# A hybrid transformer step on one core: load queues of the down phase, and the order of the first gate and up products

## The chip, the core and the metric

One core of a Trainium2 chip runs the whole kernel. The metric is the device time of one execution in microseconds (us). Its engines are TensorE (PE, with the weight loads PEld), VectorE (DVE), ScalarE (ACT), GpSimd (POOL) and SyncE (SP), each with its own instruction queue, worked off in order; they wait for one another by semaphores. DMA transfers are issued from an engine's queue (here SP, POOL and ACT) and carried by 16 DMA engines.

## The reference, cut to what matters

One layer for 512 prompt frames and 64 sample frames, 576 rows in all, D = 2048, FF = 5632, all in float32:

```
hn  = rmsnorm(x, g_norm1);  proj = hn @ w_in
mix = concat(stick-breaking attention (8 heads), gated short convolution), each normed
x   = x + mix @ w_out
h2  = rmsnorm(x, g_norm2)
y   = x + (silu(h2 @ w_gate) * (h2 @ w_up)) @ w_down
```

Outputs are y, the new keys and values and the new convolution state. The change lies in the last two lines, the feed-forward part (from about 930 us to the end).

## The kernel before

**Numbers in two parts.** Every float32 operand is held as a high part (cast to the matmul's fp32r form by ACT) and a low part (the difference, by DVE); `split` (L217, L218) makes both. A product of two operands takes three matmuls: high by high, low by high, high by low (`multiply`).

**Units.** The gate and up products are made of 42 units (numbers 0 to 41; a gate unit and an up unit for each pair of 128-wide frames of the hidden layer but the first, which the `wide` section does in the plain way). The down product has 36 units (42 to 77), listed in `DOWN`: unit (d, a, b) adds the hidden pairs a to b-1 to output column block d (256 wide), so a block is done in several units, and its running sum ("residual", x2) goes to DRAM after each unit and comes back for the next of that block. A unit is a 2 x 2 block product by Winograd's form of Strassen's method: seven products, called (n, p) for unit n and product p, of m pairs of 128 rows each, 3 m matmuls in each. A gate or up unit has m = 8, 24 matmuls in a product; a down unit m = 3 to 7.

**Order.** The matmuls run in a list written out by hand, `order`. Within a unit the products go 1, 2, 6, 7, 5, 3, 4, and product 1 of the next unit is put ahead of products 3 and 4 of this one. The operand of a product (weight columns or sums of them, L1050 to L1054, then `split` into `whl`) is prepared two products ahead (`AHEAD = 2`); DVE and ACT work in the order that the scheduler gave. Product 6 needs three sums of 128 x 1024 on DVE first. Results: products 1, 6, 5 and 3 of a unit pile up in the PSUM tile `psy`, whose states are copied out by ACT (`part`, L1074); product 2 is `psx`, 7 and 4 are `psw`. In a down unit DVE adds them to the residual tile (`add`, L1133).

**Loads.** Weights come from DRAM by SP (`load_weight`, L179) into two buffers each of `raw` and `raw2`; one unit ahead. A load waits until DVE and ACT have read the buffer. The three tiles of frames `h2a` (high, low) and `b22`, used by gate and up units, are reused in the down phase as three of seven slots; the other four slots are made when the down phase begins.

**Frames.** The frame sums (`frame_sums`, `tsum`) are made for the gate and up units while the wide section runs. Each hidden pair's seven forms are split by `put_form` (tile `form`, two buffers) and stored to `hid_dram` by POOL (L921, 288 KB each). The down phase loads a whole pair (seven forms, 2016 KB) back into a slot by SP (`load_pair`, L1139). Before, slots 0 to 3 are asked for at the start of unit 42, one more at the start of each of the next three units, and the others where `calls` says, after product 4 of a unit whose end frees slots: sometimes several at once.

**Residuals and outputs.** `load_x2` (L1124, 576 KB, SP) brings a unit's residual into one of two buffers at the start of the unit; `store_x2` (L1128, 576 KB, POOL) writes it after product 4. A load therefore waits for the store of two units before to land. The last unit of a block transposes its residual on PE and writes `ob` to the output by SP (L1155) and `obs` by ACT (L1162).

So in the down phase SP's queue holds weights, slots, residual loads and outputs, in program order; POOL's holds the form stores that are left from unit 41 and the residual stores.

Of the kernel before, what the change touches and what calls it, by code (L numbers as in the profile page):

```python
# [10 lines left out]
F32 = mybir.dt.float32  # L11
# [5 lines left out]
P = 128  # L17
# [3 lines left out]
HALF = T // 2  # L21
# [72 lines left out]
def tile_hybrid_stream_step(  # L94
# [6 lines left out]
    nc = tc.nc  # L101
# [5 lines left out]
    yp, ys = y_prompt[0], y_sample[0]  # L107
# [16 lines left out]
    specs = []  # L124
# [20 lines left out]
    NGU = len(UNITS)  # L145
# [26 lines left out]
        nc.scalar.copy(out=hi[:, a:b], in_=raw[:, a:b])  # L172
        lo_eng.tensor_tensor(out=lo[:, a:b], in0=raw[:, a:b], in1=hi[:, a:b].bitcast(F32), op=ALU.subtract)  # L173

    raws = []

    def load_weight():
        raw, raw3, src = weight_raw(len(raws))
        nc.sync.dma_start(out=raw3, in_=src)  # L179
        raws.append(raw)  # L180

    def split_weight(lo_eng):
        raw = raws[len(ready)]
# [175 lines left out]
    stores = []  # L359
    with tc.manual_schedule(engines={mybir.EngineType.Activation, mybir.EngineType.DVE, mybir.EngineType.SP}):  # L360
        raw, raw3, src = weight_raw(0)
        raws.append(raw)
        hi, lo = weight_split(0)
        w0h, w0l = ready[0]

        def load_w0(q):
            nc.sync.dma_start(out=raw3[:, 4 * q : 4 * q + 4, :], in_=src[:, 4 * q : 4 * q + 4, :])

        load_x(0)
        load_s(0)  # L370
        nc.sync.dma_start(out=g1raw, in_=g_norm1[0].rearrange("(r c) -> r c", c=P))
        load_x(1)
        load_x(2)
        load_w0(0)
        load_x(3)
        load_s(1)
        load_w0(1)
        load_x(4)
        load_s(2)
        load_x(5)  # L380
        load_w0(2)
        load_x(6)
        load_w0(3)
        load_weight()
        hi1, lo1 = weight_split(1)
        q0ps = [ps_pj.tile([P, HALF], F32, tag="pj", name="pj") for _ in HALVES]
        for kt in range(KD + LAG):
            if kt == 14:
                load_vectors()
            if kt == KD - 1:  # L390
                load_weight()
                for kt_, st in stores:
                    nc.sync.dma_start(out=xt_dram[kt_], in_=st)
                stores.clear()
            for sc, (k0, k1) in enumerate(SCH):
                if kt == k0:
                    pss, psc = turn_samples(sc), sc
            if kt == 0:
                psg = misc("ps_g1")
                nc.tensor.transpose(psg[:, :KD], g1raw, ident[:KD, :KD])  # L400
                nc.vector.tensor_copy(out=g1c, in_=psg[:, :KD])
            for c, (k0, k1) in enumerate(XCH):
                if k0 <= kt < k1:
                    turn_x(kt, c, kt - k0, psc, pss)
            if kt in (0, 4, 8, 12):
                weight_parts(raw, hi, lo, kt * P, (kt + 4) * P, nc.gpsimd if kt else nc.vector)
            if kt in (14, 16):
                a = (kt - 14) * 512
                weight_parts(raws[1], hi1, lo1, a, a + 1024, nc.gpsimd if kt == 14 else nc.vector)
            if kt >= 4 and not (kt >= 9 and kt % 2) and kt != 14 and squares and XCH[squares[0][0]][1] <= kt:  # L410
                square(*squares.pop(0))
            if kt >= LAG:
                for ps, (a, b) in zip(q0ps, HALVES):
                    step(ps, w0h, w0l, slice(0, P), xhi, xlo, kt - LAG, KD, a, b)
        pos[0] = 1
        while squares:
            square(*squares.pop(0))
        nc.sync.dma_start(out=xt_dram[KD - 1], in_=stores[0][1])
        turn_vectors()

        ssr = rpool.tile([P, 5], F32, name="ssr")
        nc.vector.reduce_sum(out=ssr, in_=ssx, axis=mybir.AxisListType.X)
        nc.vector.tensor_scalar(out=ssr, in0=ssr, scalar1=1.0 / D, scalar2=EPS, op0=ALU.mult, op1=ALU.add)
        rst = rpool.tile([P, 5], F32, name="rst")
        nc.gpsimd.tensor_tensor(out=rst, in0=ssr, in1=nhalf, op=ALU.pow)
# [467 lines left out]
    def frame_sums():  # L893

        for j in range(NP):
            ev, od = x2(2 * j), x2(2 * j + 1)
            ge, go = col("g2", 2 * j), col("g2", 2 * j + 1)
            pool, tag = (tpool, f"t{j}") if j < 4 else (ypool, f"y{j - 4}")
            b11 = tmp.tile([P, HALF], F32, tag="ms", name="b11", bufs=1)
            b22 = tmp.tile([P, HALF], F32, tag="t", name="b22", bufs=1)  # L900
            nc.scalar.activation(out=b11, in_=ev[:, :HALF], func=AF.Copy, scale=ge)
            nc.scalar.activation(out=b22, in_=od[:, HALF:], func=AF.Copy, scale=go)
            t = b12pool.tile([P, 4, HALF], F32, tag="ht", name="t")
            t1, t2, t3, t4 = (t[:, n] for n in range(4))
            nc.vector.scalar_tensor_tensor(out=t1, in0=ev[:, HALF:], scalar=ge, in1=b11, op0=ALU.mult, op1=ALU.subtract)
            nc.vector.tensor_tensor(out=t2, in0=b22, in1=t1, op=ALU.subtract)
            nc.vector.scalar_tensor_tensor(out=t3, in0=ev[:, HALF:], scalar=ge, in1=b22, op0=ALU.mult, op1=ALU.subtract)
            nc.vector.scalar_tensor_tensor(out=t4, in0=od[:, :HALF], scalar=go, in1=t2, op0=ALU.mult, op1=ALU.subtract)
            tt = pool.tile([P, 2, 4, HALF], F32R, tag=tag, name=f"tsum{j}")
            split(tt[:, 0], tt[:, 1], t)  # L910
            tsum.append(tt)
            yield 9

# [72 lines left out]

    pipe.spawn(frame_sums(), 20)
    wide("gate", row_scale2)
    load_weight()
    wide("up")  # L990
    pipe.flush()
    b12pool.release()
    blocks["pool"] = w2pool = tc.alloc_tile_pool(name="w2pool", bufs=1, reuse_waits="tile", side="left")
# [6 lines left out]
    slots = {}  # L1000
# [11 lines left out]
        return [(tsum[j][:, 0, q, :], tsum[j][:, 1, q, :]) for j in range(m)]  # L1012

    NU = len(UNITS)
    order = [(0, 1), (0, 2), (1, 1), (0, 6), (0, 7), (0, 5), (1, 2), (0, 3), (0, 4), (1, 6), (1, 7), (1, 5)]
    for n in range(1, NU):
        if n == NGU - 1:

# [13 lines left out]
    slot_turn = [0]  # L1032

    def column(i, m):
        while len(raws) <= i:
            load_weight()
        v = raws[i].rearrange("p (j s c) -> p j s c", s=2, c=P)
        return v[:, :, 0, :], v[:, :, 1, :]

# [81 lines left out]
    def load_x2(n):  # L1121
        d = UNITS[n][1]
        xt2[n] = down["pool"].tile([P, 2, T], F32, tag="x2", name=f"x2_{n}", bufs=2)
        nc.sync.dma_start(out=xt2[n], in_=x2_dram[2 * d : 2 * d + 2].rearrange("k p t -> p k t"))  # L1124

    def store_x2(n):
        d = UNITS[n][1]
# [7 lines left out]
    def load_pair(p):  # L1135
        tag = ("h2ah", "h2al", "b22", "s3", "s4", "s5", "s6")[p % SLOTS]
        pool = h2pool if p % SLOTS < 3 else down["pool"]
        slots[p] = pool.tile([P, FORMS, 2, HALF], F32R, tag=tag, name=f"slot{p}")
        nc.sync.dma_start(out=slots[p].bitcast(F32), in_=hid_dram[p])  # L1139

    def store_y(n, c, i):

        x2t, cs = xt2[n][:, c, :], slice((2 * UNITS[n][1] + c) * P, (2 * UNITS[n][1] + c + 1) * P)
        whole = (c, 1 - i) in unit[n].setdefault("done", set())
        unit[n]["done"].add((c, i))
        b0, b1 = ((0, 2), (3, 4), (0, 3), (2, 4))[2 * whole + i]

        def work():
            yield 3
            ob = down["pool"].tile([P, 3, P], F32, tag="ob", name="ob", bufs=2)[:, : b1 - b0]  # L1150
            po = misc("pot")[:, : (b1 - b0) * P]
            for q in range(b0, b1):
                nc.tensor.transpose(po[:, (q - b0) * P : (q - b0 + 1) * P], x2t[:, q * P : (q + 1) * P], ident)
            nc.vector.tensor_copy(out=ob, in_=po.rearrange("p (i c) -> p i c", c=P))
            nc.sync.dma_start(out=yp[b0 * P : b1 * P, cs].rearrange("(i p) c -> p i c", p=P), in_=ob)  # L1155
            if i:
                po2 = misc("pot2")
                nc.tensor.transpose(po2[:TS, :P], x2t[:, TP:], ident)
                os_ = down["pool"].tile([TS, P], F32, tag="obs", name="obs", bufs=2)
                nc.scalar.copy(out=os_, in_=po2[:TS, :P])  # L1160
                nc.scalar.dma_start(out=ys[:, cs], in_=os_)

        pipe.spawn(work())
# [3 lines left out]
        prepare(*order[k_])  # L1167
    for k_, (n, p_) in enumerate(order):
        if p_ == 1:
            while len(raws) < min(first_block + 2 * (n + 1) + 2, len(specs)):  # L1170
                load_weight()
        if (n, p_) == (NGU, 1):
            tpool.release()
            ypool.release()
            down["pool"] = tc.alloc_tile_pool(name="dpool", bufs=1, reuse_waits="tile", side="right")
            for p in range(3):
                load_pair(p)
            load_x2(n)
            load_pair(3)
        if n > NGU and p_ == 1:  # L1180
# [3 lines left out]
        if k_ + AHEAD < len(order):  # L1184
            prepare(*order[k_ + AHEAD])
        run(n, p_)
        if n >= NGU and p_ == 4:
            for p in calls[n - NGU]:
                load_pair(p)
# [35 lines left out]
```

## Time and profile before

| what | value |
| --- | --- |
| time, median of 3 runs | 2490.04 us (2489.23 to 2496.96) |
| profiled execution | 2492.62 us, span 2490.9 us |
| mean granted TensorE clock | 0.988 |
| DMA packets | 453122, 369.52 MB, mean 148 GB/s over the span |
| hardware queue (SP's and ACT's) | 304.24 MB, 40.3% of 16 engines' span |
| software queue (POOL's) | 61.94 MB, 6.3% |
| chain that ended last | PE 53%, issue 35%, DMA 4% |

The span is the time from the first to the last instruction of the profiled execution; 1.7 us lie around it. The chain that ended last is followed back from the end, at each step to what released it; "issue" is time in which an engine waited for nothing the profile shows, as where the chain runs along another engine's queue. Times in rows are us from the start of the span. The granted clock is the TensorE clock that was granted by the chip, 1.00 being full. A DMA's time to landing runs from its issue to the completion that its reader waits for.

### The profile page before, as it was taken

Reading aid. Unit: us, or ns where it says so; the run is one execution under the profiler, and the core shown is the slowest. Engines: PE = TensorE matmul, PEld = TensorE weight load, DVE = VectorE, ACT = ScalarE, POOL = GpSimd, SP = SyncE. Lnnn points to the kernel's source line nnn. Section 1 sums busy time; section 2 is a strip of 40 time slices with the busy share of each in tenths; the row PEclk is TensorE's granted clock in tenths of the full one; section 3 lists DMA queues with packets and bytes.
Section 4 is the critical chain, followed back from the end, with each engine's and each line's share of the span. In section 5 each row is a group of like instructions: output and inputs, shape, how many; then the busy total and the mean of one; then the engine's idle time right before and its main releaser. Section 6 shows DMA issues by size and latency. Waiting matters only on the chain.

```text
span 2490.9 us, 43942 instructions
## 1 busy us (share of the span) xinstructions
PE 2427.2 (97%) x18121; PEld 2414.4 (97%) x18121; DVE 1757.3 (71%) x2764; ACT 1069.6 (43%) x1855; POOL 222.2 (9%) x393
## 2 busy tenths in 40 slices
PE   8999999999999999999999999999999898999898
PEld 8999999999999999999999999999999898999898
DVE  7766666353345457888888888888887786777676
ACT  6655565231132344444444444444444343434333
POOL 2111010110020120001001010010100000000000
PEclk9999999999999999999999999999999898999999
DMA  8232322222242233434444444443445868768753
GB/s 267 83 91 87 91 79 86 77 85 86 85 159 74 101 132 119 140 118 149 144 145 145 125 149 145 145 151 117 152 145 186 318 197 289 255 213 289 269 150 99
DMA packets 453122, 369.52 MB, mean 148 GB/s; under 512 B 9855, under 2 KB 420089, under 8 KB 450105
## 3 DMA queue, kind: packets, MB, share of 16 engines
q1 hardware_dynamic: 435288, 304.24, 40.3%
q0 software_dynamic: 16352, 61.94, 6.3%
q8 instruction: 142, 2.33, 0.4%
q10 hardware_dynamic: 1280, 0.53, 0.1%
q14 instruction: 60, 0.48, 0.1%
HBM read 285.85 MB, written 80.82 MB: 147 GB/s over the span
## 4 chain that ended last, share of the span: by engine, by line
PE 53%; issue 35%; DMA 4%; POOL 3%; DVE 3%; ACT 1%; SPq 0%; POOLq 0%; ACTq 0%; DVEq 0%
PE pj L209 23%; PE psy L1064 10%; PE pjo L209 8%; PE psw L1064 5%; POOL hid_dram L921 3%; PE psx L1064 2%; DMA raw<-in_w_down_dram 2%; DMA slot<-hid_dram 1%; DMA hid_dram<-form 1%; PE z L547 1%; PE pw L979 1%; PE po L613 1%; DVE whl L218 0%; PE os L643 0%; PE zs L573 0%
## 5 line engine op out<-in xcount | busy, mean ns | idle before, releaser
L218 DVE TENSOR_TENSOR whl<-raw,whl 128x1024 fp32r<-128x1024 f32 (+5 forms) x468 | 481.7, 1031 | 106.2 <-ACT whl L217 104.9
L217 ACT CAST whl<-raw 128x1024 fp32r<-128x1024 f32 (+5 forms) x468 | 418.7, 897 | 285.6 <-issue 108.4
L209 PE MATMUL pj<-xhi,whi 128*128 128x288 f32 x1504 | 450.6, 300 | 0.4 <-ACT whi L172 0.4
L209 PE MATMUL pj<-xlo,whi 128*128 128x288 f32 x1504 | 444.6, 296 | 1.7 <-DVE xlo L343 1.7
L209 PE MATMUL pj<-xhi,wlo 128*128 128x288 f32 x1504 | 444.3, 295 | 0.3 <-DVE wlo L173 0.3
L1064 PE MATMUL psy<-slot,whl 128*128 128x288 f32 x2112 | 307.3, 301 | 37.1 <-DMA slot<-hid_dram 14.2
L1064 PEld LDWEIGHTS psy<-slot,whl 128*128 128x128 f32 x2112 | 292.9, 193 | 40.8 <-DMA slot<-hid_dram 15.3
L1064 PE MATMUL psy<-tsum,whl 128*128 128x288 f32 x2016 | 283.6, 297 | 7.7 <-ACT whl L217 6.3
L209 PEld LDWEIGHTS pj<-xlo,whi 128*128 128x128 f32 x1504 | 283.9, 189 | 2.0 <-DVE xlo L343 2.0
L209 PEld LDWEIGHTS pj<-xhi,whi 128*128 128x128 f32 x1504 | 284.3, 189 | 1.0 <-ACT whi L172 0.6
L209 PEld LDWEIGHTS pj<-xhi,wlo 128*128 128x128 f32 x1504 | 284.4, 189 | 0.9 <-DVE wlo L173 0.5
L1064 PEld LDWEIGHTS psy<-tsum,whl 128*128 128x128 f32 x2016 | 274.1, 190 | 8.2 <-ACT whl L217 6.6
L1064 PE MATMUL psw<-tsum,whl 128*128 128x288 f32 x2016 | 281.0, 295 | 0.0
L1064 PEld LDWEIGHTS psw<-tsum,whl 128*128 128x128 f32 x2016 | 271.8, 188 | 0.0
L172 ACT CAST whi<-raw 128x1024 fp32r<-128x1024 f32 (+1 forms) x138 | 140.2, 1031 | 231.4 <-PE pj L209 95.8
L1074 ACT COPY part<-psy 128x288 f32<-128x288 f32 x234 | 93.5, 399 | 306.2 <-PE psy L1064 298.6
L173 DVE TENSOR_TENSOR wlo<-raw,whi 128x1024 fp32r<-128x1024 f32 (+1 forms) x132 | 160.4, 1227 | 24.1 <-ACT whi L172 22.8
L921 POOL DMA_DIRECT2D hid_dram<-form x154 | 83.5, 542 | 928.6 <-DVE form L218 764.7
L1064 PE MATMUL psw<-slot,whl 128*128 128x288 f32 x1056 | 156.2, 299 | 0.0
L1064 PEld LDWEIGHTS psw<-slot,whl 128*128 128x128 f32 x1056 | 146.9, 191 | 0.0
L1064 PE MATMUL psy<-b,whl 128*128 128x288 f32 x1008 | 140.2, 295 | 0.0
L1064 PEld LDWEIGHTS psy<-b,whl 128*128 128x128 f32 x1008 | 136.0, 188 | 0.0
(331 smaller groups left out, 4142.2 us busy)
## 6 DMA issues: line engine op xcount, KB each, us to landing
raw<-in_w_in_dram SPq DMA_DIRECT2D x47, 1024.0 KB, 5.5
raw<-in_w_gate_dram SPq DMA_DIRECT2D x44, 1024.0 KB, 5.8
raw<-in_w_up_dram SPq DMA_DIRECT2D x44, 1024.0 KB, 6.2
hid_dram<-form POOLq DMA_DIRECT2D x154, 288.0 KB, 2.6
slot<-hid_dram SPq DMA_DIRECT2D x22, 2016.0 KB, 10.9
x<-x_dram SPq DMA_DIRECT2D x36, 576.0 KB, 4.0
raw<-in_w_down_dram SPq DMA_DIRECT2D x30, 640.0 KB, 6.2
raw<-in_w_out_dram SPq DMA_DIRECT2D x16, 1024.0 KB, 5.3
```

The source lines that it names most:

```text
L172: nc.scalar.copy(out=hi[:, a:b], in_=raw[:, a:b])
L173: lo_eng.tensor_tensor(out=lo[:, a:b], in0=raw[:, a:b], in1=hi[:, a:b].bitcast(F32), op=ALU.subtract)
L209: mm(ps, w_[:, k, csl], x_[:, k, a:b], start=(k == 0 and n == 0), stop=(k == nk - 1 and n == 2))
L217: nc.scalar.copy(out=hi, in_=src)
L218: (lo_eng or nc.vector).tensor_tensor(out=lo, in0=src, in1=hi.bitcast(F32), op=ALU.subtract)
L547: mm(zb[i], a_[:, kk], b_[:, q0:TP], start=(n == 0), stop=False, skip_group_check=True)
L613: mm(po[:, i * P : 512], a_[:, i, :], b_[:, : 512 - i * P], stop=(i == 0 and n == 2), **kw)
L921: nc.gpsimd.dma_start(out=hid_dram[fp][:, n - 1], in_=t.bitcast(F32))
L979: mm(pss[j, i], w_[:, k, j * P : (j + 1) * P], x_, start=(kk == 0 and k == 0 and n == 0), stop=(kk == 1 and k == 7 and n == 2))
L1064: mm(ps, whl[:, w_, j, :], x_, start=(start and j == 0 and q == 0), stop=(j == len(xs_) - 1 and q == 2), skip_group_check=True)
L1074: nc.scalar.copy(out=t, in_=st["y"])
```

## The change

- `raws` becomes a dictionary and `load_weight` can be told which weight to load. The first weights of units 0 and 1 come while `wide("up")` runs: `first_block` ahead of it, `first_block + 2` in the middle of it. The order of the loads on SP stays: first weight of unit 0, first of unit 1, second of unit 0, second of unit 1.
- `order` begins (0,1), (0,2), (1,1), (1,2), (0,6), (0,7), (0,5), (0,3), (0,4): product 2 of unit 1 comes ahead of four products of unit 0, which it followed.
- `frame_sums` holds its four sums in two tiles, and splits each pair of sums by itself: operations of 576 elements in place of 1152.
- Residual loads, slots and outputs are issued by POOL in place of SP. Nothing but weights is left on SP in the down phase.
- Slots 0 and 1 are asked for after product (41, 2), slot 2 after (41, 3), in place of the start of unit 42. Slot 3 and the later ones keep their places in the program.

POOL's queue in the down phase is then: slots 0 to 2 with the last form stores between them, residual of unit 42, slot 3, two form stores, residual of 43, slot 4, and so on; later, for a burst, slot 7, store of residual 50, slots 8, 9 and 10, residual load 52, store 51, residual load 53.

```
-    raws = []
+    raws = {}
-    def load_weight():
-        raw, raw3, src = weight_raw(len(raws))
+    def load_weight(i=None):
+        i = len(raws) if i is None else i
+        raws[i], raw3, src = weight_raw(i)
         nc.sync.dma_start(out=raw3, in_=src)
...
-            t = b12pool.tile([P, 4, HALF], F32, tag="ht", name="t")
-            t1, t2, t3, t4 = (t[:, n] for n in range(4))
+            ta = b12pool.tile([P, 2, HALF], F32, tag="ta", name="ta")
+            tb = b12pool.tile([P, 2, HALF], F32, tag="tb", name="tb")
+            t1, t2, t3, t4 = ta[:, 0], ta[:, 1], tb[:, 0], tb[:, 1]
...
-            split(tt[:, 0], tt[:, 1], t)
+            split(tt[:, 0, :2], tt[:, 1, :2], ta)
+            split(tt[:, 0, 2:], tt[:, 1, 2:], tb)
...
     wide("gate", row_scale2)
-    load_weight()
-    wide("up")
+    load_weight(first_block)
+    wide("up", lambda: load_weight(first_block + 2))
...
-    order = [(0, 1), (0, 2), (1, 1), (0, 6), (0, 7), (0, 5), (1, 2), (0, 3), (0, 4), (1, 6), (1, 7), (1, 5)]
+    order = [(0, 1), (0, 2), (1, 1), (1, 2), (0, 6), (0, 7), (0, 5), (0, 3), (0, 4), (1, 6), (1, 7), (1, 5)]
...
     def load_x2(n):
-        nc.sync.dma_start(out=xt2[n], in_=x2_dram[2 * d : 2 * d + 2].rearrange("k p t -> p k t"))
+        nc.gpsimd.dma_start(out=xt2[n], in_=x2_dram[2 * d : 2 * d + 2].rearrange("k p t -> p k t"))
     def load_pair(p):
-        nc.sync.dma_start(out=slots[p].bitcast(F32), in_=hid_dram[p])
+        nc.gpsimd.dma_start(out=slots[p].bitcast(F32), in_=hid_dram[p])
     def store_y(n, c, i):
-            nc.sync.dma_start(out=yp[b0 * P : b1 * P, cs].rearrange("(i p) c -> p i c", p=P), in_=ob)
+            nc.gpsimd.dma_start(out=yp[b0 * P : b1 * P, cs].rearrange("(i p) c -> p i c", p=P), in_=ob)
...
         if p_ == 1:
-            while len(raws) < min(first_block + 2 * (n + 1) + 2, len(specs)):
-                load_weight()
+            for i in range(first_block + 2 * n, min(first_block + 2 * n + 4, len(specs))):
+                if i not in raws:
+                    load_weight(i)
         if (n, p_) == (NGU, 1):
...
-            for p in range(3):
-                load_pair(p)
             load_x2(n)
             load_pair(3)
...
         run(n, p_)
+        if n == NGU - 1:
+            for p in {2: (0, 1), 3: (2,)}.get(p_, ()):
+                load_pair(p)
         if n >= NGU and p_ == 4:
             for p in calls[n - NGU]:
                 load_pair(p)
```

More of the change, by code (lines that the diff above doesn't have):

```diff
@@ L173, in weight_parts @@
         lo_eng.tensor_tensor(out=lo[:, a:b], in0=raw[:, a:b], in1=hi[:, a:b].bitcast(F32), op=ALU.subtract)
-    raws = []
-    def load_weight():
-        raw, raw3, src = weight_raw(len(raws))
+    raws = {}
+    def load_weight(i=None):
+        i = len(raws) if i is None else i
+        raws[i], raw3, src = weight_raw(i)
         nc.sync.dma_start(out=raw3, in_=src)
-        raws.append(raw)
     def split_weight(lo_eng):
@@ L361, in tile_hybrid_stream_step @@
         raw, raw3, src = weight_raw(0)
-        raws.append(raw)
+        raws[0] = raw
         hi, lo = weight_split(0)
@@ L1034, in column @@
     def column(i, m):
-        while len(raws) <= i:
-            load_weight()
+        if i not in raws:
+            load_weight(i)
         v = raws[i].rearrange("p (j s c) -> p j s c", s=2, c=P)
@@ L1169, in tile_hybrid_stream_step @@
         if p_ == 1:
-            while len(raws) < min(first_block + 2 * (n + 1) + 2, len(specs)):
-                load_weight()
+            for i in range(first_block + 2 * n, min(first_block + 2 * n + 4, len(specs))):
+                if i not in raws:
+                    load_weight(i)
         if (n, p_) == (NGU, 1):
```

## The prediction

> **What bounds the kernel now.** I read the page's totals first, then the waits of TensorE in the stretch from 1900 us on, then the windows that cut the span where PE falls short.
>
> ```profile
> PE 2427.2 (97%) x18121; PEld 2414.4 (97%) x18121; DVE 1757.3 (71%) x2764; ACT 1069.6 (43%) x1855; POOL 222.2 (9%) x393
> PE psy L1064 <- DMA slot<-hid_dram: 14.2, 3, 7.0
> PE psy L1064 <- ACT whl L217: 10.5, 1, 10.5
> PE psy L1064 <- ACT part L1074: 6.7, 3, 6.0
> PE psy L1064 <- DVE whl L218: 5.2, 5, 3.2
> 990.00:1005.00 15.00, 7.32 (x36) 6.77 (x36) 12.81 (x16) 5.92 (x9) 2.16 (x4) 0.67 0.36 124
> 1925.00:1950.00 25.00, 11.99 (x62) 11.40 (x61) 12.41 (x28) 5.54 (x14) 3.05 (x6) 0.68 0.72 289
> 1950.00:2058.00 108.00, 108.00 (x809) 108.00 (x809) 88.86 (x158) 48.59 (x88) 5.87 (x9) 1.00 0.78 255
> 2058.00:2088.00 30.00, 19.21 (x123) 18.42 (x123) 14.68 (x28) 7.78 (x16) 1.33 (x2) 0.77 1.02 389
> 2155.00:2203.00 48.00, 42.38 (x300) 40.98 (x300) 31.72 (x51) 16.97 (x28) 2.16 (x3) 0.97 0.80 266
> 2320.00:2350.00 30.00, 23.18 (x152) 22.70 (x151) 20.27 (x30) 8.98 (x15) 1.44 (x2) 0.83 0.79 283
> ```
>
> TensorE is the bound: 97% busy, and 100% in the quiet stretch 1950 to 2058, where 809 matmuls take 108.00 us, 0.1335 us each. The columns of a window are its length, then busy time and count of PE, PEld, DVE, ACT and POOL, then granted clock, DMA share and GB/s. What the change can win is therefore only where PE stands still or runs at a low clock. Length less count times 0.1335 gives both together. Entry into the gate/up units (990): 15 - 36 x 0.1335 = 10.2 us. Entry into the down phase (S1, 1925): 25 - 8.3 = 16.7. The burst of four slots (S2, 2058): 30 - 16.4 = 13.6. S3 (2155): 48 - 40.1 = 8.0. S4 (2320): 30 - 20.3 = 9.7. Together **58.2 us**, the most that the change can win; beside the 97% that looks like nothing, and it is 2.3% of the span. The clock column matters: it falls to 0.67 to 0.83 in just these windows, so a stall costs more than its own length, here 58.2 against the 15.0 + 25.0 + 30.0 + 48.0 + 30.0 less PE busy of 104.1, which is 43.9.
>
> Next, what ended those stalls: the chain of waits, and the timelines of SP and POOL.
>
> ```profile
> 2059.92 21.50 DMA raw<-in_w_down_dram
> 2329.42 11.25 DMA slot<-hid_dram
> 1934.96 7.86 DMA hid_dram<-form
> 2156.63 7.85 DMA raw<-in_w_down_dram
> 2185.65 12.09 DMA raw<-in_w_down_dram
> 1925.00 0.34 SPq L1139 DMA_DIRECT2D slot<-hid_dram  x1
> 2054.01 2.13 SPq L1139 DMA_DIRECT2D slot<-hid_dram  x4
> 2059.92 16.41 SPq L179 DMA_DIRECT2D raw<-in_w_down_dram  x2
> 2076.42 3.53 SPq L1124 DMA_DIRECT2D x<-x_dram  x1
> 2155.66 0.37 SPq L1124 DMA_DIRECT2D x<-x_dram  x1
> 2156.12 1.09 SPq L179 DMA_DIRECT2D raw<-in_w_down_dram  x2
> 2184.68 0.37 SPq L1124 DMA_DIRECT2D x<-x_dram  x1
> 2185.14 2.47 SPq L179 DMA_DIRECT2D raw<-in_w_down_dram  x2
> 2325.30 4.03 SPq L1124 DMA_DIRECT2D x<-x_dram  x1
> 2329.42 0.44 SPq L1139 DMA_DIRECT2D slot<-hid_dram  x1
> DMA to landing us min/median/max: 7.6/10.9/24.7
> DMA to landing us min/median/max: 2.4/2.6/8.7
> DMA to landing us min/median/max: 3.3/4.5/11.8
> ```
>
> The last three rows are the landing times of the slots, of the frame (form) stores, and of the residual loads and stores together. In S2 SP issues four slots of 2016 KB at 2054.01 and then weights at 2059.92, which land 21.50 us later, and SP itself is held 16.41 us before it can issue a residual load. In S3 and S4 SP stands at a residual load (which waits for the store of the buffer's last user) and only then issues what is late: weights at 2156.12, the last slot at 2329.42. So the five stalls are of two kinds, **order** (S3, S4) and **bandwidth** (S1, S2: the DMA share is 1.02 in S2).
>
> **The change part by part.**
>
> *Entry.* Product (1,2) is pulled ahead of (0,6), (0,7) and (0,5): 24 matmuls, 24 x 0.1335 = 3.2 us, moved into the wait for the operand of (0,6).
>
> ```profile
> PE psy L1064 <- ACT whl L217: 6.3, 1, 6.3
> L218 DVE TENSOR_TENSOR tsum<-t,tsum x8: 1346/1358/1360, 935.9 to 981.6; 128x1152 fp32r<-128x1152 f32 x8
> 984.18 7.85 DMA hid_dram<-form
> 993.34 1.22 DVE L1050 TENSOR_TENSOR s<-raw 128x1024 f32<-128x1024 f32 x1
> 994.59 1.23 DVE L1051 TENSOR_TENSOR raw<-raw,raw 128x1024 f32<-128x1024 f32 x1
> 998.45 0.61 PE L1064 MATMUL psy<-tsum,whl 128*128 128x288 f32 x1 [6.33 <-ACT whl L217]
> ```
>
> PE waits 6.33 us, until 998.45, because the sums behind (0,6), L1050 and L1051, come on DVE after the frames of the wide section, which wait for a frame store (7.85 us). With (1,2) first PE works to about 995.3. But (1,2) also puts a cast and a difference of 128 x 1024 (1.2 us of DVE) ahead of those sums, and the split of tsum in two makes eight operations of 1.36 us into sixteen on DVE, and as many on ACT. From 1.22 us at 1024 elements (L1050) and 1.36 at 1152, 0.0011 us an element, I estimate 0.73 for 576, so 8 x (1.46 - 1.36) = 0.8 us more on DVE, while its first half can start sooner. They lie between 935.9 and 983, where PE is full; I cost them at nothing, and at 0.8 us if the last of them delays the sums. The operand then comes between 995 and 999, a stall of 0 to 3.5 and something at low clock. I put the loss at 3.5 (0 to 8) instead of 10.2: **-6.7**.
>
> *S1.* Slots 0 and 1 are issued after (41,2), slot 2 after (41,3), on POOL. Slot 2 takes the buffer of b22, which (41,3) reads last, so its issue, at 1925.00, does not move; what moves is what is in flight beside it. Alone a slot takes 7.6 us: 1932.6. PE is through the first two slots at about 1928.9 (1927.97 + 0.97) and got slot 2 at 1935.9, so the first stall shrinks from 6.97 to about 3.7. The second (6.04 us, a copy on ACT that stood behind a frame cast, which waited for a frame store of 7.86 us) mostly goes, since slot 3 is now queued behind those stores and not beside them.
>
> ```profile
> 1927.97 0.97 PE L1064 MATMUL psy<-slot,whl 128*128 128x288 f32 x6
> 1935.91 1.09 PE L1064 MATMUL psy<-slot,whl 128*128 128x288 f32 x3 [6.97 <-DMA slot<-hid_dram]
> 1945.19 2.53 PE L1064 MATMUL psy<-slot,whl 128*128 128x288 f32 x9 [6.04 <-ACT part L1074]
> ```
>
> Against that, slot 3 comes later by the two frame stores, and the first weights must still arrive beside two slots. 3.7 and 2 of stall and 3.3 of low clock (before: 13.0 of stall, 3.7 of clock): 9 (5 to 16) instead of 16.7: **-7.7**.
>
> *S2.* The weights leave the queue of the slots, so they need not wait behind four. But the engines are full: 2016 KB are 2.06 MB, at that window's 389 GB/s 5.3 us, so four slots last from 2054 to 2075, and two weights of 640 KB another 3.4 us, whatever the order. The residual of the unit, now issued on POOL behind slots 8 to 10, comes about then too; before it was issued at 2076.42. DVE has in its order the work for two more products ahead of that residual's sum, so it isn't late for PE at once. Weights at about 2078 instead of 2081.4: 10 (5 to 16) instead of 13.6: **-3.6**.
>
> The Trainium skill, "DMA: Bandwidth & Descriptors", Queues, rings and completion order, says that an engine takes turns between its queue rows packet by packet; so a weight's small packet goes after each slot packet, and by that rule the weights would creep until the slots end. The trace agrees as far as it reaches: a frame store beside slots took up to 8.7 us, against 2.4 at least. The same page, Issuing engines are not separate DMA queues, says that spreading transfers over issuing engines saves only issue time; by it this stage would win nothing (13.6 stays).
>
> *S3 and S4.* On SP nothing but weights is left, whose only wait is for DVE to free their buffers. The weights of 2156.12 and 2185.14 no longer stand behind a residual load: 1.5 (0 to 5) instead of 8.0, **-6.5**. The last slot (21) waited for SP from 2325.30 to 2329.42; on POOL it stands behind the store of a residual which was issued at 2326.22, and can be issued by 2327. At 7.6 us it lands at 2334.5 instead of 2340.7, the stall falls from 6.3 to about 1: 2.5 (1 to 9) instead of 9.7, **-7.2**.
>
> ```profile
> 2326.22 0.71 POOL L1128 DMA_DIRECT2D x_dram<-x  x1 [11.15 <-DVE x L1133]
> L921 POOL DMA_DIRECT2D hid_dram<-form x154: 539/539/769, 978.5 to 1945.7; - x154
> ```
>
> *What POOL takes over.* 22 slots, 36 residual loads and the outputs: at 0.54 us (the frame store, 128 rows) to 0.72 (the residual store, 256 rows), some 58 x 0.6 = 35 us and the outputs, on an engine with 222 us of 2491 busy. Issue is free. Its order is not: POOL's queue now holds a residual's store, which waits for DVE, ahead of every later load, and each residual load lies behind the slots issued before it. Slots 16 and 20 now stand behind such a store. In units 43 to 45, each with a slot, a residual (576 KB, 1.5 us at the 389 GB/s) can start when the store two units before has landed, and then lies behind a slot of 5.3: I estimate it some 3 us late for the matmuls that it is added to, which the lead of the operands (two products, 2 x 12 x 0.1335 = 3.2 us of PE at four pairs) about covers. I put **+2** (0 to 57, see the third rival). The outputs at the end change issuer, not order: 0 (-2 to +2), the gaps after 2450 stay.
>
> The Trainium skill, "SBUF — State Buffer", in its warning on DVE and SWDGE, says that DMAs issued by GpSimd can be held while VectorE copies in a two-port mode; the frame stores' issue of 539 ns, median and least, with 769 at most, beside a DVE at 71%, shows no such hold before, and no run here shows it for slots.
>
> **Sum.** -6.7 - 7.7 - 3.6 - 6.5 - 7.2 + 2 = -29.7 us. The profiled execution took 2492.6 (span 2490.9 and 1.7 around it), which gives 2462.9; it lies 2.6 above the median of 2490.04, and the same gain from the median gives 2460.3. I predict **2460**. All low ends of the losses (0 + 5 + 5 + 0 + 1 = 11) give 2490 - 47 = 2443; all high ends (8 + 16 + 16 + 5 + 9 = 54) leave 4 us of gain, 2486.
>
> **Rivals.** *1. Order only.* Where the engines are full, moving the issue wins nothing: S1 and S2 stay at 16.7 and 13.6, entry, S3 and S4 gain 20.4, less 2: about **2472** (2465 to 2482). For it: the DMA share of 1.02 in S2. Against it: the second stall of S1 hangs on a store beside slots, not on the total.
>
> *2. The change does not free the weights.* Their buffers are freed by DVE late, so that they are issued when they were before (at 2059.92 they were issued 0.03 us after such a sum), or slots and weights still hold each other: only the entry is won, less the extra order on POOL: **2485** (2482 to 2494). Against it: 2156.12 and 2329.42 come right behind a residual load.
>
> *3. Slower: residuals behind slots.* A residual load lies in one queue with the slots and lands a slot later, and DVE, in order, holds the next operands behind its sum. The place is the 13 units that have a slot right ahead of their residual on POOL (43 to 45, 52, and nine around slots 11 to 21). A slot costs 7.6 us less the 3.2 us of lead, 4.4, and it decides from the point where the residual lands over 3.2 us after its product: 13 x 4.4 = 57, less 29.7 + 2: 2490 + 25 = **2515** (2498 to 2530). For it: landings up to 24.7 us. Against it: a unit of four pairs lasts 84 x 0.1335 = 11.2 us, and a slot with a residual load and store takes 5.3 + 2 x 1.5 = 8.3 of the line.
>
> **How the numbers follow.** Forecast 0.53 (2443 to 2470), rival 1 0.27, rival 2 0.07, rival 3 0.13. A measurement of this kernel tells about 0.3%, 7.5 us, from no change: faster below 2482.5, slower above 2497.5. Forecast, rival 1 and a bit of 2 are faster: 0.81; the rest of 2 and the edge of 3: same 0.06; slower 0.13. The range leaves out rival 3 and a few in a hundred below: 2443 to 2488.
>
> **What would show it.** Entry: (1,2) between (1,1) and (0,6), and a stall under 4 us. S1: one stall of about 4 us on slot 2 and none of 6 on the copy. S2: weights landing at about 18 us after issue, not 21.5; if PE waits there for DVE's residual sum, rival 3 is at work. S3: weights issued within 1 us of DVE's release, landing in 3 us; S4: slot 21 landing under 8 us after issue and PE waiting 1 us. Wrong would be: PE waits ended by the residual's sum in units 43 to 45 or 52, or a POOL queue that stands at a store while a free slot waits for it.

## The result, and the profile after

| | median, us | lowest to highest | runs |
| --- | --- | --- | --- |
| before | 2491.35 | 2489.23 to 2496.96 | 6 |
| changed | 2512.01 | 2503.42 to 2514.22 | 6 |

The ratio is 1.0071 (95% interval 1.0051 to 1.0092): slower, where 2460 was forecast, and outside the range of 2443 to 2488. The profiled execution took 2504.79 us (span 2503.1), 12.2 more than the profiled one of before; two more profiled executions of the same kernel took 2504.92 and 2506.47. So the traces show 12 of the 21 us between the medians; the rest lies in executions that left no trace.

First the same windows as in the prediction, shifted where the changed kernel is later: entry, S1, S2, S3, S4 and the end (columns as there).

```profile
985.00:1012.00 27.00, 22.56 (x155) 21.89 (x154) 21.95 (x29) 10.39 (x16) 2.71 (x5) 0.94 0.62 190
1895.00:1995.00 100.00, 78.80 (x542) 77.30 (x541) 58.66 (x108) 33.60 (x65) 13.48 (x22) 0.91 0.73 265
2058.00:2108.00 50.00, 32.63 (x220) 31.94 (x219) 25.84 (x49) 13.08 (x26) 6.52 (x10) 0.83 0.79 287
2160.00:2215.00 55.00, 55.00 (x415) 55.00 (x414) 45.98 (x70) 24.30 (x39) 6.12 (x9) 1.00 0.89 287
2310.00:2370.00 60.00, 46.70 (x333) 45.66 (x332) 39.09 (x64) 19.33 (x34) 7.41 (x11) 0.89 0.71 251
2370.00:2503.00 133.00, 122.77 (x918) 119.99 (x916) 94.85 (x157) 47.71 (x86) 25.52 (x37) 0.99 0.45 129
```

The stalls of the changed kernel are longer than the prediction's windows, so here are windows of before of like extent, for the same sum:

```profile
985.00:1012.00 27.00, 19.32 (x125) 18.77 (x124) 19.24 (x23) 9.05 (x14) 2.16 (x4) 0.81 0.49 152
1895.00:1985.00 90.00, 76.99 (x547) 76.40 (x547) 60.37 (x107) 33.97 (x64) 6.50 (x11) 0.91 0.78 281
2050.00:2100.00 50.00, 39.21 (x273) 38.42 (x273) 31.20 (x58) 17.29 (x35) 2.14 (x3) 0.86 0.85 309
2150.00:2205.00 55.00, 49.38 (x351) 47.98 (x350) 38.65 (x62) 19.54 (x35) 2.16 (x3) 0.97 0.79 261
2300.00:2360.00 60.00, 52.80 (x372) 52.08 (x372) 42.53 (x70) 21.65 (x38) 2.86 (x4) 0.91 0.80 280
2360.00:2491.00 131.00, 121.38 (x909) 118.70 (x907) 94.39 (x156) 46.73 (x84) 0.00 (x0) 1.00 0.46 127
```

Length less matmuls times 0.1335 us, as in the prediction:

| stage | before | after | measured | forecast |
| --- | --- | --- | --- | --- |
| entry | 10.3 | 6.3 | -4.0 | -6.7 |
| S1 | 17.0 | 27.6 | +10.6 | -7.7 |
| S2 | 13.6 | 20.6 | +7.0 | -3.6 |
| S3 | 8.1 | 0 | -8.1 | -6.5 |
| S4 | 10.3 | 15.5 | +5.2 | -7.2 |
| end | 9.6 | 10.4 | +0.8 | 0 |

They add up to +11.5, against 12.2 of span. (The forecast's sum held another +2 for POOL, for the residual loads of units 43 to 45; they lie in S1.) The forecast had the stages right, and in the entry and S3 the gain; in S1, S2 and S4 it had the wrong sign. What PE waits for there is told by the waits of PE and DVE over 900 (PE) or 1900 (DVE) to the end, first those of the changed kernel, then DVE's waits for weights and residuals in the kernel before:

```profile
PE psy L1066 <- ACT part L1076: 20.8, 5, 13.8
PE psy L1066 <- DVE whl L218: 19.1, 5, 9.3
PE psy L1066 <- DMA slot<-hid_dram: 8.8, 2, 7.3
DVE s L1052 <- DMA raw<-in_w_down_dram: 70.2, 14, 17.4
DVE x L1135 <- DMA x<-x_dram: 2.0, 1, 2.0
```

```profile
DVE s L1050 <- DMA raw<-in_w_down_dram: 31.5, 14, 7.5
DVE x L1133 <- DMA x<-x_dram: 3.7, 4, 1.5
```

DVE's wait for weights (L1050 of before is L1052 after) more than doubles, 31.5 to 70.2 us, while it waits 2.0 us for residuals (3.7 before). PE's waits for DVE's operands and ACT's copies hang on it, as the chain of waits of the changed kernel shows (start, us, what):

```profile
1907.48 13.32 DMA raw<-in_w_down_dram
...
1943.93 20.48 DMA raw<-in_w_down_dram
...
2066.09 23.94 DMA raw<-in_w_down_dram
2090.03 0.02 issue
2090.05 0.04 ACTq L217
2090.09 0.04 issue
2090.13 0.04 ACT whl L217
2090.17 0.09 issue
2090.26 0.02 ACTq L217
2090.28 0.38 issue
2090.66 0.40 ACT part L1076
2091.06 0.04 issue
2091.10 6.50 PE psy L1066 x36
...
2326.29 21.60 DMA raw<-in_w_down_dram
```

Weights that took 3.3 us at least take 13 to 24 here, each time while a slot is under way. (In S2 the kernel before had 21.5 already, as the prediction shows.) In S2 the rows in between show how a late weight reaches PE: ACT stands at the cast of a weight, and the copy of psy behind it, which PE needs for the next product, is 13.8 us late. And the DMA view of 2072 to 2082, inside the burst of slots, shows why:

```profile
DMA packets 571, 4.24 MB, mean 424 GB/s; under 512 B 32, under 2 KB 317, under 8 KB 317
q0 software_dynamic: 285, 4.08, 95.6%
q1 hardware_dynamic: 285, 0.15, 4.8%
```

Queue 0 is POOL's, with the slots, queue 1 SP's, which holds only weights. In 10 us each got 285 packets: one for one. But a slot's packet is a row of 16128 bytes and a weight's one of 512, so the weights got 0.15 MB of 4.24, 3.5%. The turn was the same from 1914 to 1918, 108 packets to 107. It was not from 1956 to 1960, inside the 20.48 us of the weight issued at 1943.93; there SP's queue got still less, and why isn't known:

```profile
q0 software_dynamic: 115, 1.73, 100.9%
q1 hardware_dynamic: 16, 0.01, 0.7%
```

### The profile page after: what moved, and what is told of

Read it like the earlier page. It is cut to its first block, busy times and chain, and to the rows that moved or that the text cites. A ratio compares the mean times of both kernels' runs of the same rounds, so it can differ in the third digit from the quotient of the medians.

```text
span 2503.1 us, 43901 instructions
## 1 busy us (share of the span) xinstructions
PE 2425.3 (97%) x18121; PEld 2412.5 (96%) x18121; DVE 1756.5 (70%) x2772; ACT 1070.0 (43%) x1863; POOL 282.8 (11%) x483
## 4 chain that ended last, share of the span: by engine, by line
PE 88%; DMA 5%; issue 3%; DVE 2%; ACT 1%; POOL 0%; SPq 0%; POOLq 0%; DVEq 0%; ACTq 0%
PE psy L1066 29%; PE pj L209 23%; PE psw L1066 15%; PE pjo L209 8%; PE psx L1066 7%; DMA raw<-in_w_down_dram 4%; PE pw L981 2%; DVE whl L218 1%; PE z L547 1%; PE po L613 1%; DMA xin<-in_x_prompt_dram 0%; DVE x L1135 0%; DMA slot<-hid_dram 0%; PE os L643 0%; PE zs L573 0%
## 5 line engine op out<-in xcount | busy, mean ns | idle before, releaser
L1066 PEld LDWEIGHTS psy<-slot,whl 128*128 128x128 f32 x2112 | 291.2, 192 | 49.9 <-ACT part L1076 21.3
L1066 PE MATMUL psx<-h2ah,whl 128*128 128x288 f32 x672 | 135.6, 297 | 2.7 <-DVE gs L960 2.7
## 6 DMA issues: line engine op xcount, KB each, us to landing
slot<-hid_dram POOLq DMA_DIRECT2D x22, 2016.0 KB, 10.5
```

Source lines behind the costliest of these rows:

```text
L1066: mm(ps, whl[:, w_, j, :], x_, start=(start and j == 0 and q == 0), stop=(j == len(xs_) - 1 and q == 2), skip_group_check=True)
```

## The experiments

Theory 1: weights in another queue than the slots are starved beside them (kept waiting by the other queue's traffic), by that turn packet for packet; in one queue a weight that is issued first goes first. Theory 2, the prediction's third rival: residual loads lie behind slots in POOL's queue. Theory 2's sign had come true and nearly its time, 2515, so it had to be tested as well. All ratios are to the kernel before on the same chip, with the 95% interval.

| run | what | median, us | ratio |
| --- | --- | --- | --- |
| e1 | entry edits alone | 2488.61 | 0.9987 (0.9977 to 0.9996) |
| e2 | before, slots on POOL | 2504.21 | 1.0049 (1.0032 to 1.0066) |
| e3 | before, residual loads on POOL | 2493.3 | 1.0003 (0.9994 to 1.0013) |
| e4 | changed, slots on SP | 2489.22 | 0.9987 (0.9978 to 0.9997) |
| e5 | changed, slots in seven transfers | 2504.19 | 1.0051 (1.0032 to 1.0071) |
| e6 | changed, residual loads on SP | 2502.54 | 1.0044 (1.0029 to 1.0059) |
| e7 | e1, burst dealt out | 2481.17 | 0.9961 (0.9947 to 0.9975) |
| e8 | e7, slots in seven transfers on SP | 2468.5 | 0.9909 (0.9894 to 0.9924) |
| e9 | changed, slots 0 to 2 late | 2506.32 | 1.0061 (1.0042 to 1.0081) |
| e10 | e8 with the burst in one | 2474.93 | 0.993 (0.991 to 0.9949) |
| e11 | e8, residual loads on POOL | 2466.35 | 0.9886 (0.9867 to 0.9905) |
| e12 | e8, slots 0 to 2 early | 2470.01 | 0.9899 (0.9881 to 0.9917) |

**e1, entry edits alone.** The changed kernel with L1126, L1141 and L1157 back on `nc.sync` and slots 0 to 2 back at the start of unit 42.

> The changed kernel with its down phase as before (slots, residual loads and outputs on SP, slots 0 to 2 at the start of unit 42); the entry edits alone stay. Both theories of the down phase say the same here: the entry loses 6.6 us in the changed kernel's trace and 10.7 before, so about 4 us less than before, 2487 (2483 to 2491). If it is slower than before, the entry edits carry part of the loss.

2488.61, as expected: the entry edits win 0.13%, some 3 us. The loss is in the down phase.

**e2 and e3, one issuer alone**, each one line of the kernel before:

```
-        nc.sync.dma_start(out=slots[p].bitcast(F32), in_=hid_dram[p])
+        nc.gpsimd.dma_start(out=slots[p].bitcast(F32), in_=hid_dram[p])
```

```
-        nc.sync.dma_start(out=xt2[n], ...)
+        nc.gpsimd.dma_start(out=xt2[n], ...)
```

> The kernel before with nothing changed but the issuer of the slots: POOL in place of SP. Theory 1 (starved weights: where weights and slots lie in two queues, a weight gets one small packet for each large packet of a slot, so that a weight issued before or beside a slot lands only when the slot is through): slower than before, 2500 to 2515, with weights landing 12 us and more after issue beside each slot, and PE waiting for operands in S1 and S4. Theory 2 (residual loads behind slots in POOL's queue; my third rival): the residual loads are on SP here, so no loss, 2480 to 2492.

> The kernel before with nothing changed but the issuer of the residual loads: POOL in place of SP; slots stay in the queue of the weights. Theory 1: no starving, and SP is no longer held at a residual load, so S3 and S4 shrink: 2470 to 2482. Theory 2: here residual loads stand in POOL's queue behind residual stores only, not behind slots, so it gives the same; if it is slower than before, the order of POOL's queue is what costs.

e2: slower by 0.49%, with the residual loads on SP. Its chain shows the same weights, and DVE's wait for them:

```profile
1953.16 18.16 DMA raw<-in_w_down_dram
...
2072.92 22.36 DMA raw<-in_w_down_dram
```

```profile
DVE s L1050 <- DMA raw<-in_w_down_dram: 61.1, 14, 15.7
DVE x L1133 <- DMA x<-x_dram: 13.4, 8, 5.5
```

The time is the one that theory 1 gave, and theory 2 can't make this loss. In its burst, from 2080 to 2090, POOL's queue and SP's got 286 packets each again, and SP's 0.15 MB of 4.26. Its trace is of the slowest of its executions (2514.14 us). The residual loads, which share SP's queue with the weights here, come late as well: DVE waits 13.4 us for them, 3.7 before.

e3: no change, where theory 1 as I had put it expected 2470 to 2482: a miss. In its trace, which is of its slowest execution (2497.95 us), S3 is gone, as intended, but S1 has grown, and in the down phase as a whole DVE now waits for residuals:

```profile
1895.00:1995.00 100.00, 81.11 (x552) 79.83 (x552) 62.84 (x112) 33.96 (x65) 10.71 (x17) 0.88 0.74 266
2160.00:2215.00 55.00, 55.00 (x415) 55.00 (x414) 46.15 (x70) 24.38 (x39) 5.04 (x7) 1.00 0.87 283
```

```profile
DVE x L1133 <- DMA x<-x_dram: 30.2, 5, 14.7
```

S1 loses 100 - 552 x 0.1335 = 26.3 us (before 17.0). DVE waits 30.2 us for residuals over the down phase, 3.7 before, and 12.8 us for weights, 31.5 before. So it isn't only weights: in e2 the weights and here the residuals, taken out of the slots' queue, are waited for longer. What is won in S3 is lost again in S1. But only 6.3 of the 30.2 us lie in S1; the longest wait of DVE there is one for the casts of frames on ACT (18.5 us, 12.5 before), so that the residuals alone make S1's growth is not shown.

**e4, the changed kernel with its slots on SP** (one line, L1141).

> The changed kernel with only the slots put back on SP, the queue of the weights (early slots 0 to 2 stay early; residual loads and outputs on POOL). Theory 1: the 48 us of PE waiting in S1, S2 and S4 fall to 25 or less: 2465 to 2480, faster than both kernels. Theory 2: the same side, since the residuals no longer lie behind slots, but the weights' landing times beside slots would be as in the changed kernel (12 to 24 us).

2489.22, against 2512 for the changed kernel in its own comparison: putting the slots back takes the whole loss away, but no more than the entry's gain is left; 2465 to 2480 was expected. Its windows show it to be like e3: S3 at 0.5, S1 still at 24.7. DVE waits as in e3 too, 14.5 us for weights (70.2 in the changed kernel) and 30.7 for residuals (2.0).

```profile
1895.00:1995.00 100.00, 82.02 (x564) 80.97 (x563) 63.93 (x115) 34.83 (x66) 9.60 (x15) 0.88 0.78 279
2155.00:2210.00 55.00, 54.35 (x408) 54.12 (x407) 44.53 (x67) 23.30 (x37) 5.35 (x8) 1.00 0.85 275
```

So in S1 putting the slots back wins only 27.6 - 24.7 = 2.9 us of the trace. With either move alone S1 loses 26 us (e2: 26.2; e3: 26.3), with both 27.6: they do not add up there, and starved weights are not the only way to its loss. In S2 and S4 putting the slots back wins more: e4 loses 14.8 and 7.3 us there, the changed kernel 20.6 and 15.5.

**e5, smaller packets**, and **e6, residual loads on SP**, both from the changed kernel:

```
-        nc.gpsimd.dma_start(out=slots[p].bitcast(F32), in_=hid_dram[p])
+        for f in range(FORMS):
+            nc.gpsimd.dma_start(out=slots[p][:, f].bitcast(F32), in_=hid_dram[p][:, f])
```

> The changed kernel with each slot loaded by POOL in seven transfers, one for each form, so that a slot's rows are 2304 bytes and not 16128. Theory 1 in its exact form (the DMA engines take one packet from each queue in turn, 285 of each in 10 us of the changed kernel's burst): a weight now gets 512 bytes for each 2304, so weights beside the four slots land about 10 us after issue in place of 24, and the time falls to 2485 to 2500, though there are seven times as many issues on POOL (some 3.9 us a slot). If it isn't the turn by packets but a plain preference for POOL's queue, the weights still land after the slots, and it stays at 2503 to 2520.

> The changed kernel with only the residual loads put back on SP; slots stay on POOL. Theory 1: the weights starve as they did: 2500 to 2515. Theory 2 (residual loads behind slots in POOL's queue): the cause is gone, 2470 to 2490.

e5: 2504.19, some 8 us below the changed kernel's median, but the intervals overlap, and it is 4 us above what was expected. It lies in the range of the other reading, a plain preference for POOL's queue. The view of 2066 to 2076, in its burst, shows that the share of the weights did rise:

```profile
q0 software_dynamic: 722, 2.68, 71.5%
q1 hardware_dynamic: 1861, 0.94, 31.9%
```

0.94 MB of 3.63 is 26%, seven times the share above. It is no longer one for one (2.6 packets of SP's queue for each of POOL's), so the exact rule doesn't hold in this stretch. Nor are POOL's packets rows of 2304 bytes, as the expectation had them: 2.68 MB in 722 packets are 3.7 KB each, and 581 of them have 4608 bytes in the trace, two rows. The longest weight of the burst still took 19.96 us by its chain (expected about 10), until 2082.92. But POOL issued the last piece of the burst's slots only at 2083.00, so this weight did not wait for all of them, as a plain preference for POOL's queue would have it. S1, S2 and S4 lose 22.8, 16.8 and 12.9 us in e5's trace, 11 less in all than in the changed kernel, while DVE's wait for weights hardly fell (68.1 us, 70.2 in the changed kernel). So with smaller packets the weights' share rose and these stages lost less, but the time did not come back, and what the rest is was not settled by this run: the late weights are shown, and that packet size alone makes them late is not.

e6: slower by 0.44% with the residual loads back on SP, as theory 1 had it, and DVE still waits 52.3 us for weights. Theory 2 expected 2470 to 2490 and falls as the main cause. It may add something: 1.0071 less 1.0044 is 0.27%, with intervals that overlap.

**e7 to e12, towards a better version.** e7 is e1 with one line in `down_calls`; e8 adds the seven transfers, on SP:

```
+    calls[8:11] = [7], [8, 9], [10]
```

```
-        nc.sync.dma_start(out=slots[p].bitcast(F32), in_=hid_dram[p])
+        for f in (0, 1, 5, 6, 4, 2, 3):
+            nc.sync.dma_start(out=slots[p][:, f].bitcast(F32), in_=hid_dram[p][:, f])
```

> The entry edits with the down phase as before (the run of entry edits alone gave 2488.6), and the burst of four slots after unit 50 dealt out: slot 7 after unit 50, slots 8 and 9 after 51, slot 10 after 52. Weights and residuals then lie between slots in SP's queue. If the stall at 2070 is a matter of 2016 KB times four ahead of the weights, whatever the queue, it falls from 13 to 5 us or less: 2476 to 2483. If the bandwidth over the whole stretch is short, the stall only moves: 2486 to 2491.

> As the spread one, and each slot loaded on SP in seven transfers, in the order in which the products use the forms, so that frame stores and residual stores on POOL's queue share with packets of 2304 bytes and not of 16128, and product 1 can start on its own form. By theory 1, stores beside slots land sooner (frame stores 4 us or less in place of 7 to 9), S1 shrinks from 16 to 8 or less: 2466 to 2478. If packet size is not what decides, as the spread one or slower by the issue time on SP (seven times 0.34 us a slot).

e7 gives 2481.17, within its range: the stall at 2070 was a matter of four slots ahead of the weights (2045 to 2115 loses 3.0 us in its trace, 13.7 in e1's). e8 gives 2468.5, within its range and better than both kernels. PE's waits for slots over 900 to the end are, in e7 and in e8:

```profile
PE psy L1067 <- DMA slot<-hid_dram: 13.4, 3, 6.7
```

```profile
PE psy L1067 <- DMA slot<-hid_dram: 4.9, 2, 3.2
```

The expectation that frame stores would land in 4 us or less missed: between 1900 and 1960 e8's took 5.7 to 6.5, e1's 2.4 to 8.2 with a median of 6.4. S1 shrank all the same, to 6.3 us (17.0 before), so the time was right and the reason given for it was not. Whether e8 gains by the smaller packets or by starting a product on its own form was not separated.

> The changed kernel with slots 0 to 2 asked for at the start of unit 42 again, still on POOL. If the early slots are what starves the first weights in S1 (weights landing 11 to 13 us after issue at 1907 to 1911, and 3.1 us of PE waiting before 1923), the time falls by those 3 to 5 us and the later starving stays: 2503 to 2511. If early slots help on the whole, it is slower than the changed kernel's 2512: 2513 to 2520.

e9 gives 2506.32, within its 2503 to 2511, but its interval overlaps that of the changed kernel: that the early slots cost is not shown.

> Slots in seven transfers of one form on SP (the entry edits stay, the down phase else as before), with the burst of four slots after unit 50 in one again. The run with both gave 2468.5, the spread alone 2481.2. If the two are separate gains of about 12.7 (small transfers) and 7.4 (spread), this gives 2488.6 - 12.7 = 2476 (2472 to 2480); if the spread does nothing more once the slots come in forms, 2468 to 2471.

e10 gives 2474.93, near the 2476 of two separate gains. But the ratios of e8 and e10 overlap in their intervals, so what dealing out adds to the seven transfers is not clear of the noise; between 2045 and 2115 the traces lose 7.1 us in e8 and 16.1 in e10.

> The best version so far (slots by forms on SP, spread, 2468.5) with the residual loads alone on POOL, which was one aim of the change: SP is then never held at a residual load. Theory 1: with packets of like size the residuals are not starved by slots, so that this may now pay for S3 and S4: 2460 to 2468. If a load that is in another queue than the slots loses by it in any case, it is slower than 2468.5: 2470 to 2480.

> The best version so far (slots by forms on SP, spread) with slots 0 to 2 asked for early as in the change, after products (41,2) and (41,3), now in the queue of the weights. In one queue the first weights lie behind two slots of 5.3 us; they were issued some 5 us before they were needed: a loss of up to 5 us, 2468 to 2474, if the weights decide; a gain of up to 4 us, 2464 to 2468, if the slots do.

e11 gives 2466.35 and e12 2470.01; neither can be told from e8's 2468.5, so neither question is settled. In e11's trace DVE waits 21.3 us for residuals, 1.4 in e8's: a queue of their own still makes it wait longer for them, also where the slots come in small pieces.

**e13 and e14, the changed kernel again.**

> The changed kernel once more, for a second profile. Its timed executions lie between 2503 and 2514 us and the first profiled one at 2504.8, so the first trace shows 12 of the 21 us only. Theory 1 expects the rest in the same places (weights beside slots in S1, S2 and S4, 30 us and more of PE waiting in S1); if it lies elsewhere, in the gate and up units or at the end, there is a cause that the first trace doesn't show.

> The same kernel a third time, for the spread of the stalls between executions: theory 1 expects S3 near nothing each time, and S1, S2 and S4 together at 60 us or more.

Both gave about the time of the first profiled execution, with the stalls in the same places: in e14 S1 loses 100 - 540 x 0.1335 = 27.9 us, S3 nothing, and S1, S2 and S4 together 65, as expected. The larger stall that was looked for in S1 (30 us of PE waiting) is in neither.

```profile
1895.00:1995.00 100.00, 79.37 (x540) 77.57 (x540) 58.46 (x107) 32.48 (x62) 13.49 (x22) 0.91 0.73 266
2160.00:2215.00 55.00, 55.00 (x414) 55.00 (x414) 45.80 (x69) 24.13 (x40) 6.36 (x10) 1.00 0.88 286
```

No profiled execution fell at the 2510 to 2514 that four of the timed ones took, so where those 6 to 9 us more lie stays open.

## Why the prediction was wrong, point by point

- *What bounds the kernel* held: the stages named are those that moved.
- *Entry*: the mechanism was right. The term was 6.7 us and measured 4.0; e1 alone gave 3 us. PE's first new wait is one for DVE to read a gate result out of PSUM (2.7 us), which the prediction did not count, and after it comes the operand's (1.2 us, 6.3 before).
- *S3* was right: SP is no longer held at a residual load, -8.1 against -6.5. But in e3, which makes the same gain by the residual loads alone, S1 loses 9.3 us more than before, so that the time stays.
- *S1, S2 and S4* failed, above all at one step: "On SP nothing but weights is left, whose only wait is for DVE to free their buffers." The weights were costed by when they can be issued, not by when they land. They are issued early and then land 13 to 24 us later; in the burst's 10 us they got 3.5% of the bytes. S1's price named only that "the first weights must still arrive beside two slots", and S4's counted on slot 21 alone. In S1 the waits of PE, 13.0 us before, were 21.2: 7.6 for late operands, 7.3 for slot 2 (3.7 forecast, since the slot took 9.18 us and not 7.6), 3.5 for the copy that was to go, and 2.8 for a read of PSUM by DVE. That the weights alone make this stage's loss is not shown: e4 keeps most of it.
- The same step in another form: in S2 the prediction says that weights "would creep until the slots end", by the Trainium skill, "DMA: Bandwidth & Descriptors", Queues, rings and completion order, and then used it for S2 only. The trace agrees with that rule in the slots' burst, 285 packets against 285, and not everywhere (115 against 16 from 1956 to 1960). Taken to every place where a slot and a weight are under way together (1907, 1943, 2066, 2326) it gives the sign of the result, and it should have been a rival of its own. The other sentence that the prediction took from the Trainium skill, "DMA: Bandwidth & Descriptors", Issuing engines are not separate DMA queues, that spreading transfers over issuing engines saves only issue time, is too mild here: e2 changed nothing but the issuer of the slots and lost 0.49%.
- *S2* besides: "whatever the order" was nearly right, since before and after the weights land behind four slots (21.5 and 23.94 us). The two weights are of 512 KB, not of 640, a slip of 0.7 us in the price. PE's wait for the late weight grew only from 10.5 to 13.8 us; 1.4 for a slot and 2.2 for a residual's sum came to it. That sum is the sign which the prediction gave for its third rival, but DVE's queue had been held 17.4 us by a weight before it, and by no residual. Slots 8 to 10 waited for a residual store on POOL in addition, and came 4.3 us behind slot 7:

```profile
2060.47 0.57 POOL L1141 DMA_DIRECT2D slot<-hid_dram  x1 [6.35 <-PE psw L1066]
2064.08 0.71 POOL L1130 DMA_DIRECT2D x_dram<-x  x1 [3.04 <-DVE x L1135]
2064.79 1.65 POOL L1141 DMA_DIRECT2D slot<-hid_dram  x3
```

- *S4*: "at 7.6 us it lands at 2334.5": what ended the wait was not slot 21 but a weight, 21.60 us after its issue at 2326.29. Slot 21 itself took 12.5 us.
- *The rivals*: the third had the sign and nearly the time (2515), but by luck, since it had not the cause: DVE waits 2.0 us for residuals in the changed kernel, and with the residual loads on SP (e6) the loss is still 0.44%. The first (order only, 2472) failed too: S1 and S2 did not stay, they grew.

## What to carry to other kernels

Before a stream is moved to a queue of its own, ask what it runs beside and how large the packets on each side are: in the slots' burst a queue of 512-byte rows beside one of 16128-byte rows got 3.5% of the bytes. One queue is also an order of urgency: a small urgent load can be issued ahead of a large one, and here that was worth more than a queue that is never held (e2 against the kernel before, e4 against the changed one). What paid was to make the large transfers smaller and to deal them out in the same queue (e8: 2468.5 us, 0.9% below the kernel before, entry edits included).

## What the runs showed of the hardware that was not expected

- Between two queues the share went by packets where one had rows of 16128 bytes (285 to 285 in 10 us of the changed kernel, 286 to 286 in e2), but not one for one with 2304-byte rows on POOL (722 to 1861), where the packets held 3.7 KB on average.
- Frame stores beside slots landed hardly sooner in the median when the slots came in rows of 2304 bytes on SP (5.9 us against 6.4).
- The changed kernel's six timed executions spread over 11 us (2503 to 2514), the four of e8 over 3 (2467.64 to 2470.85).
